# Two of four column groups of an output projection as a seven-product pair, on one Trainium2 core

## The chip, the cores and the metric

The kernel runs on one core of one Trainium2 chip. The metric is device time in microseconds (us); a median of several runs is compared. The engines are TensorE (PE in the profile), VectorE (DVE), ScalarE (ACT), GpSimd (POOL) and SyncE (SP, whose queue issues the plain loads).

## The reference

One layer of a streaming encoder on 256 tokens of width 2048 in float32: a SwiGLU block with layer norm, a mixer with two branches, a second SwiGLU block, and a gated per-layer embedding. The change lies in the last part of the mixer and touches the norm behind it:

```
merged = sigmoid(ga) * (y_m @ w_up_m) + sigmoid(gb) * (y_sb @ w_up_sb)   # (256, 2048)
mix    = merged @ w_out                                                  # w_out: 2048 x 2048
x      = layer_norm(ALPHA * x + mix)
```

## The kernel before

**Products.** Every float32 operand of a large product is cut into a high part in the fast matmul format (a cast on ScalarE, L1275) and the rest (a subtraction on VectorE, L1279); a product is then three matmuls, high by high, high by low and low by high (L1331 to L1333). A *weight* is a raw tile of 256 rows by 512 columns, loaded by SP (L1249) and split into two tiles. A *unit* is one weight against one token tile of 128 tokens, so six matmuls of 512 columns. Activations lie transposed in an `ActT`, in four chunks of 512 rows and two token tiles.

**Two ways to multiply.** `group` (L344) is the classical way: 512 output columns over all 2048 rows are eight weights, each used by two units, 16 units in all. `both7` (L420) takes two groups of 512 columns at once by `seven` (L354): in each of four quarters of the rows, a two-by-two block product (two token tiles, two column groups, two halves of rows) is made with seven products instead of eight. Each of the seven has a weight of its own with a single unit. Products 1 and 2 use the plain activations with two plain weights; products 5, 7, 6 and 3 use sums of the activations, called *forms*; 4 uses the plain ones. The weight of 5 is that of 1 plus another, made in place, that of 7 also a sum: where a quarter is in `loaded`, both are made by an accumulating load from GpSimd (L377), issued when the weight whose tile they overwrite or build on has been split. The sums for 6 and 4 are made on VectorE (L371). Results leave PSUM as sums and differences (`put`, L425, and L431).

**Forms.** An `ActT` that is built with a second one as `forms` keeps a whole copy of each transposed chunk (a second copy on ScalarE), and `form_turn` (L310) makes the sums: four half-size operations on VectorE (L315 to L319), then a cast and a subtraction for each of two tiles.

**The order.** The program is one written list of units. `Sched` holds delayed pieces of work (transposes, forms, norms) with due times in a modelled clock that advances with the units; they are put into the engines' queues between units when they come due. `weave` spreads a side list evenly by columns between the units of a main list. `skewed` puts all units of the first token tile ahead of those of the second. Splits are put out ahead of use as far as `limits` (L1231) allows: `HELD` gives for each mode how many raw tiles and how many split weights may be held. Near a boundary the limits are 4 and 11. Everything of 4 KB a partition (raw tiles, split tiles, activations, x, gates, norm weights) is a page of one pool of 51; a piece of work without a free page waits until one is given back.

**The stage.** Before the stage runs a woven part (mode "woven": 9 raw, 6 split) whose side list is of seven-product pairs, the last of them `pair(3)`, and whose main list ends with `ups(2)`. Then, in mode "mix" (6 and 6), x is brought back, the six merge turns of the first three chunks come due (`merge_turn`, L1086: transposes L298, a copy L300 and a subtraction L305), and `ups(3)`, 16 units, makes the last chunk of `merged`: `up_done` multiplies by the gate (L1079) and adds the halves (L1081). After that come four classical groups of w_out. Each result is added to ALPHA times x (L1134), with statistics for the norm (L501). The last six weights of the last group are skewed, so that the norm of the first token tile (L507 to L513, transposes L524, L292, L293) runs beside the last units of the second. Behind the boundary comes the second SwiGLU block.

Of the kernel before, what the change touches and what calls it, by code (L numbers as in the profile page):

```python
# [13 lines left out]
P = 128  # L14
S = 256
TT = S // P
D = 2048
# [6 lines left out]
COL = 512  # L24
# [2 lines left out]
TEMP_BUFS = 6  # L27


HELD = {"ffn": (11, 6), "mix": (6, 6), "woven": (9, 6), "wide": (11, 6)}  # L30
RAW_EDGE, SPLIT_EDGE = 4, 11
EDGE = 6

AHEAD = 3
PSUM_BUFS = 8
SKEW = 6

HEAD = 20

# [13 lines left out]


DELAY = {
    "alpha": 24.0, "away": 5.0, "sig": 5.0, "form": 18.0, "ln_turn": 3.6, "ln_step": 2.1, "gb": 14.0, "h": 8.0, "silu": 6.0, "late": 9.0, "last": 5.0, "rest": 1.2, "mt": 3.2,
    "sbt": 4.6, "g0": 3.0, "g1": 4.0, "g2": 12.0, "cv0": 1.0, "cv1": 5.0, "cv2": 1.3,
    "m0": 4.0, "m1": 4.0, "m2": 2.0, "m3": 4.6, "m4": 4.6, "sa": 1.4, "s0": 6.5, "s1a": 4.0, "s1": 4.5, "s2": 3.0, "s3": 5.0, "s4": 5.5,
}
# [47 lines left out]
class ActT:  # L107


    def __init__(self, alloc, forms=None, later=False):  # L110
        self.alloc, self.soon = alloc, forms is not None and not later
        self.forms, self.whole = forms, {}
        self.tiles = {}
        self.left = {}

    def get(self, c, tt):
        if (c, tt) not in self.tiles:
# [62 lines left out]
def flat(pairs):  # L180
    return [u for p in pairs for u in p]


def skewed(pairs):
    return [p[0] for p in pairs] + [p[1] for p in pairs]
# [3 lines left out]
def kernel(  # L189
# [7 lines left out]
    x, out = x[0], out[0]  # L197
# [11 lines left out]
    sched = Sched()  # L209
    temps = [0]  # L210

    def temp():
        sched.until(lambda: temps[0] < TEMP_BUFS)
        temps[0] += 1
        return temp_pool.tile([P, COL], F32, name="temp", tag="temp")

    def drop(n=1):
        temps[0] -= n
# [76 lines left out]
    def transposed(src, act, c, t):  # L295
        ps = misc([P, 4, P])
        for k in range(4):
            nc.tensor.transpose(ps[:, k], src[:, k * P:(k + 1) * P], ident[:])  # L298
        dst = act.get(c, t)
        nc.scalar.copy(dst[:, 0], ps[:])  # L300
        if act.soon:
            if c not in act.whole:
                act.whole[c] = big()
            nc.scalar.copy(act.whole[c][:, t * COL:(t + 1) * COL], ps.rearrange("q k s -> q (k s)"))  # L304
        nc.vector.tensor_tensor(out=dst[:, 1], in0=ps[:], in1=dst[:, 0], op=ALU.subtract)  # L305
        act.mark(c, t, 4)
        if act.soon and all(act.ready(c, h) for h in range(TT)):
            sched.spawn(form_turn(act, c), DELAY["form"] + 5.0 * c)

    def form_turn(act, c):  # L310

        a = [act.whole[c][:, t * COL:(t + 1) * COL] for t in range(TT)]
        s12, s34 = temp(), temp()
        l, r = slice(0, 2 * P), slice(2 * P, 4 * P)
        nc.vector.tensor_tensor(out=s12[:, l], in0=a[1][:, r], in1=a[1][:, l], op=ALU.subtract)  # L315
        nc.vector.scalar_tensor_tensor(out=s12[:, r], in0=s12[:, l], scalar=-1.0, in1=a[0][:, l],  # L316
                                       op0=ALU.mult, op1=ALU.subtract)
        nc.vector.tensor_tensor(out=s34[:, l], in0=a[0][:, l], in1=a[1][:, l], op=ALU.subtract)
        nc.vector.tensor_tensor(out=s34[:, r], in0=a[0][:, r], in1=s12[:, r], op=ALU.add)  # L319
        yield 4.0  # L320
        for h, src in enumerate((s12, s34)):
            dst = act.forms.get(c, h)
            split_psum(dst[:, 0], dst[:, 1], src.rearrange("q (k s) -> q k s", s=P))
            drop()
            act.forms.mark(c, h, 4)
# [18 lines left out]
    def group(w, rows, col0, cols, act, done):  # L344

        accs = [{} for _ in range(TT)]
        pairs = []
        for i, r in enumerate(rows):
            tile = plain(rows_of(w, r, col0, cols))
            pairs.append([Unit(tile, t, accs[t], act, r // COL, r % COL // P,  # L350
                               i == 0, i == len(rows) - 1, done) for t in range(TT)])
        return pairs
# [59 lines left out]
    def in_line(pairs):  # L412

        out = []
        for head, first, then in pairs:
            at = max(len(out) - 4, 0)
            out = out[:at] + head + out[at:] + first + then
        return out

    def both7(w, ca, cb, act, dest, ready, loaded):  # L420

        r, held = {}, {}

        def put(k, t, a, b, op):
            nc.vector.tensor_tensor(out=r[k, t], in0=a, in1=b, op=op)  # L425

        def rest():
            u = r[0, 1]
            put(0, 1, held[7], u, ALU.add)
            z = r[1, 1] = dest(1, 1)  # L430
            nc.vector.scalar_tensor_tensor(out=z, in0=u, scalar=-1.0, in1=held[5],  # L431
                                           op0=ALU.mult, op1=ALU.subtract)
            ready(1, 1)
            return
            yield

        def done(m, ps):
            held[m] = ps
            if m == 1:
                r[0, 1] = dest(0, 1)  # L440
                nc.scalar.copy(r[0, 1], ps)
            elif m == 2:
                r[0, 0] = dest(0, 0)
                nc.scalar.copy(r[0, 0], ps)
                ready(0, 0)
            elif m == 6:
                r[1, 0] = dest(1, 0)
                put(0, 1, ps, r[0, 1], ALU.add)
                put(1, 0, held[5], r[0, 1], ALU.add)
                sched.spawn(rest(), DELAY["rest"])  # L450
            elif m == 4:
                sched.until(lambda: (1, 1) in r)
                put(0, 1, ps, r[0, 1], ALU.add)
                ready(0, 1)
            elif m == 3:
                put(1, 0, ps, r[1, 0], ALU.subtract)
                ready(1, 0)

        return seven(w, ca, w, cb, D, COL, act, done, loaded)
# [3 lines left out]
    def mode(name):  # L463
        program.append(Mode(name))
# [6 lines left out]
    class Norm:  # L471
# [47 lines left out]
        def turn(self, t, c):  # L519

            xs, act = xres(t, c * COL), self.act
            ps = misc([P, 4, P])
            for k in range(4):
                nc.tensor.transpose(ps[:, k], xs[:, k * P:(k + 1) * P], ident[:])  # L524
            if act.soon:
                if c not in act.whole:
                    act.whole[c] = big()
                whole = act.whole[c][:, t * COL:(t + 1) * COL]
            else:
                whole = temp()[:]  # L530
            whole = whole.rearrange("q (k s) -> q k s", s=P)
            for k in range(4):
                i = 4 * c + k
                activate(whole[:, k], ps[:, k], ACT.Identity, scale=self.gb[:, i:i + 1], bias=self.gb[:, 16 + i:17 + i])
            dst = act.get(c, t)
            split_psum(dst[:, 0], dst[:, 1], whole)
            act.mark(c, t, 4)
            if not act.soon:
                drop()
            elif all(act.ready(c, h) for h in range(TT)):  # L540
                sched.spawn(form_turn(act, c), DELAY["form"] + 5.0 * c)
            sched.spawn(self.affine(t, c), self.wait[0] + self.wait[1] * (2 * c + t))
            return
            yield
# [512 lines left out]
            yield from stick(h)  # L1057


    mergedT = ActT(act_tile)  # L1060
    ga0 = sq0 + 3 * HS * DS
    gt = {}

# [30 lines left out]
    def ups(g, swap=False):  # L1094
        parts = [flat(group(w_up_m, range(0, HM * DM, 2 * P), g * COL, COL, ymT, up_done(g, 0, swap))),
                 flat(group(w_up_sb, range(0, HS * DS, 2 * P), g * COL, COL, ysbT, up_done(g, 1, not swap)))]
        if swap:
            parts.reverse()
        return parts[0] + parts[1]
# [12 lines left out]
    def pair(g):  # L1112
# [6 lines left out]
    mode("woven")  # L1119
    program.extend(weave(main, in_line([both7(w_in, sq0 + 2 * HS * DS, sq0 + 2 * HS * DS + COL, x1T, sv_dest, sv_ready, later),  # L1120
                                   both7(w_in, 3072, 3072 + COL, x1T, mo_dest, mo_ready, every), pair(1), pair(2), pair(3)])))
    mode("mix")
    program.append(bring_back)
    program.append(lambda: [sched.spawn(merge_turn(g, t), 1.0 + 2.0 * g + t) for g in range(3) for t in range(TT)])
    program.extend(ups(3))

    x2T = ActT(act_tile, ActT(act_tile))
    norm2 = Norm(ln2_g[0], ln2_b[0], x2T, ALPHA, (4.0, 1.0))
# [1 line left out]
    def out_done(g):  # L1130
        def done(ps, t):
            assert (t, g) in norm1.whole
            xs = xres(t, g * COL)
            nc.vector.scalar_tensor_tensor(out=xs, in0=xs, scalar=ALPHA, in1=ps, op0=ALU.mult, op1=ALU.add)  # L1134
            norm2.chunk(t, g)
        return done

    for g in range(4):
        pairs = group(w_out, range(0, D, 2 * P), g * COL, COL, mergedT, out_done(g))
        if g == 3:  # L1140
            program.extend(flat(pairs[:-SKEW]) + skewed(pairs[-SKEW:]))
        else:
            program.extend(flat(pairs))
        if g == 1:
            program.append(norm2.load)

    boundary("ffn")

# [220 lines left out]
```

## Time and profile before

| | |
|---|---|
| median of 3 runs | 2165.43 us (2164.31 to 2167.08) |
| the profiled execution | 2164.03 us |
| its span | 2162.3 us |
| instructions | 27685 |
| TensorE, VectorE, ScalarE, GpSimd busy | 2153.1, 1897.6, 1344.6, 218.2 us |

Times in the views are counted from the first instruction of the span. TensorE shows as busy nearly throughout, because its matmuls are pipelined and their ends are modelled; what it does in a stretch is read from the distance of its results. A line such as L1279 collects the splits of all stages, so stages are told apart by windows of time. In the order of time of an engine, a bracket at the end of a row tells how long the engine stood before it and what released it.

### The profile page before, as it was taken

How to read it: one execution, taken by the hardware profiler on the slowest of the kernel's cores; microseconds unless marked ns; L12 is line 12 of the kernel's file. 1: busy time of each engine (PE TensorE's matmuls, PEld its weight loads, DVE VectorE, ACT ScalarE, POOL GpSimd, SP SyncE). 2: the span in 40 equal slices, each digit the busy share in tenths (PEclk: the TensorE clock that was granted, in tenths of full speed). 3: DMA queues.
4: the chain of work that ended last, by engine and by line, in shares of the span. 5: the costliest groups of instructions: out<-in, count | busy, mean ns of one | idle time of the engine just before them, and what ended most of it. 6: DMA issues, size and time to landing. Idle time of an engine off the chain costs nothing.

```text
span 2162.3 us, 27685 instructions
## 1 busy us (share of the span) xinstructions
PE 2153.1 (100%) x9798; PEld 1782.0 (82%) x9798; DVE 1897.6 (88%) x2096; ACT 1344.6 (62%) x1663; POOL 218.2 (10%) x186
## 2 busy tenths in 40 slices
PE   9999999999999999999999999999999999999999
PEld 7888888888888888888888888888888888888887
DVE  6899999999998898887888975799999999999974
ACT  7656656666665765677866563556656656666572
POOL 0111111111000000101011000011111111110000
PEclk9999999999999999999999999999999999999999
DMA  9899899999994667978898976579989999999642
GB/s 350 220 272 271 248 269 277 273 277 269 266 316 148 211 217 217 244 212 208 263 276 264 274 259 206 200 191 277 267 245 279 277 272 270 265 273 301 233 168 86
DMA packets 283179, 535.98 MB, mean 248 GB/s; under 512 B 17144, under 2 KB 34464, under 8 KB 283040
## 3 DMA queue, kind: packets, MB, share of 16 engines
q1 hardware_dynamic: 234624, 440.87, 60.0%
q0 software_dynamic: 48416, 93.33, 24.0%
q8 instruction: 77, 1.26, 0.2%
q14 instruction: 62, 0.51, 0.1%
HBM read 527.85 MB, written 6.29 MB: 247 GB/s over the span
## 4 chain that ended last, share of the span: by engine, by line
PE 91%; DVE 4%; issue 3%; DMA 2%; ACT 0%; POOL 0%; SPq 0%; DVEq 0%; POOLq 0%; ACTq 0%
PE mm L1331 29%; PE mm L1333 29%; PE mm L1332 29%; DMA raw<-in_ffn_w_dram 2%; DVE split L1279 2%; PE ms L298 1%; PE ms L524 0%; DVE actT L293 0%; POOL raw L377 0%; DVE raw L371 0%; PE ms L911 0%; PE ms L1019 0%; PE ms L989 0%; PE ms L926 0%; ACT split L1275 0%
## 5 line engine op out<-in xcount | busy, mean ns | idle before, releaser
L1275 ACT CAST split<-raw 128x1024 fp32r<-128x1024 f32 (+1 forms) x1089 | 1089.5, 1043 | 516.9 <-DMA raw<-in_ffn_w_dram 185.8
L1279 DVE TENSOR_TENSOR split<-raw,split 128x1024 fp32r<-128x1024 f32 (+1 forms) x1089 | 1277.1, 1210 | 136.6 <-ACT split L1275 128.5
L1331 PE MATMUL mm<-split,actT 128*128 128x512 f32 x3064 | 1201.2, 392 | 0.9 <-DVE actT L1025 0.9
L1333 PE MATMUL mm<-split,actT 128*128 128x512 f32 x3064 | 1187.7, 388 | 0.6 <-DVE actT L305 0.6
L1332 PE MATMUL mm<-split,actT 128*128 128x512 f32 x3064 | 1186.1, 387 | 0.4 <-DVE split L1279 0.4
L1333 PEld LDWEIGHTS mm<-split,actT 128*128 128x128 f32 x3064 | 575.1, 188 | 121.5 <-DVE actT L305 1.8
L1331 PEld LDWEIGHTS mm<-split,actT 128*128 128x128 f32 x3064 | 575.7, 188 | 115.5 <-ACT big L243 1.1
L1332 PEld LDWEIGHTS mm<-split,actT 128*128 128x128 f32 x3064 | 575.8, 188 | 114.5 <-DVE split L1279 1.7
L377 POOL DMA_DIRECT2D raw<-in_ffn_w_dram x140 | 169.7, 1440 | 1202.8 <-DVE split L1279 780.0
L371 DVE TENSOR_TENSOR raw<-raw 128x1024 f32<-128x1024 f32 x190 | 231.4, 1219 | 1.6
L377 POOL DMA_DIRECT2D raw<-in_w_in_dram x38 | 46.0, 1428 | 502.6 <-DVE split L1279 432.8
L300 ACT CAST actT<-ms 128x512 fp32r<-128x512 f32 x60 | 35.1, 586 | 73.6 <-PE ms L298 69.2
L649 DVE SCALAR_TENSOR_TENSOR big<-mm,big 128x512 f32<-128x512 f32 x112 | 76.3, 683 | 3.3 <-PE mm L1333 3.3
L597 DVE TENSOR_TENSOR temp<-mm,temp 128x512 f32<-128x512 f32 x108 | 73.1, 686 | 1.7 <-PE mm L1333 0.3
L305 DVE TENSOR_TENSOR actT<-ms,actT 128x512 fp32r<-128x512 f32 x60 | 40.9, 685 | 14.4 <-ACT big L304 9.3
L243 ACT ACTIVATE temp<-mm 128x512 f32<-128x512 f32 (+1 forms) x36 | 20.3, 569 | 49.9 <-PE mm L1333 49.9
L293 DVE TENSOR_TENSOR actT<-temp,actT 128x512 fp32r<-128x512 f32 x40 | 26.5, 687 | 17.3 <-ACT actT L292 17.2
L239 ACT ACT_TABLE_LOAD x30 | 38.5, 1283 | 0.5
L1191 DVE TENSOR_TENSOR temp<-temp,big 128x512 f32<-128x512 f32 (+1 forms) x10 | 5.8, 582 | 26.4 <-ACT temp L243 26.4
L292 ACT CAST actT<-temp 128x512 fp32r<-128x512 f32 x40 | 23.9, 620 | 8.0 <-DVE temp L316 7.4
L243 ACT ACTIVATE rstd<-mv,eps 128x1 f32<-128x1 f32 x6 | 1.8, 294 | 41.8 <-DVE mv L507 41.8
L1134 DVE SCALAR_TENSOR_TENSOR big<-big,mm 128x512 f32<-128x512 f32 x8 | 5.5, 686 | 25.3 <-PE mm L1333 25.3
(138 smaller groups left out, 613.1 us busy)
## 6 DMA issues: line engine op xcount, KB each, us to landing
raw<-in_ffn_w_dram SPq DMA_DIRECT2D x527, 512.0 KB, 7.0
raw<-in_w_in_dram SPq DMA_DIRECT2D x144, 512.0 KB, 5.1
raw<-in_ffn_w_dram POOLq DMA_DIRECT2D x140, 512.0 KB, 9.9
raw<-in_w_in_dram POOLq DMA_DIRECT2D x38, 512.0 KB, 8.4
raw<-in_w_out_dram SPq DMA_DIRECT2D x32, 512.0 KB, 5.3
raw<-in_w_ple_gate_dram SPq DMA_DIRECT2D x32, 512.0 KB, 5.0
raw<-in_w_in_dram SPq DMA_DIRECT2D x56, 256.0 KB, 4.1
raw<-in_w_up_m_dram SPq DMA_DIRECT2D x16, 512.0 KB, 6.3
```

The costliest lines, as they stand in the source:

```text
L239: nc.scalar.preload_act_table_set(table[0])
L300: nc.scalar.copy(dst[:, 0], ps[:])
L305: nc.vector.tensor_tensor(out=dst[:, 1], in0=ps[:], in1=dst[:, 0], op=ALU.subtract)
L371: nc.vector.tensor_tensor(out=out.tile[:, :, :cols], in0=a.tile[:, :, :cols], in1=b.tile[:, :, :cols], op=ALU.add)
L377: nc.gpsimd.dma_start(out=out.tile[:, :, :cols], in_=src, accum_op=ALU.add)
L597: nc.vector.tensor_tensor(out=out, in0=a, in1=b, op=op)
L649: nc.vector.scalar_tensor_tensor(out=xs, in0=ps, scalar=0.5, in1=xs, op0=ALU.mult, op1=ALU.add)
L1275: nc.scalar.copy(hi[:, ks], r[:, ks])
L1279: nc.vector.tensor_tensor(out=lo[:, ks], in0=r[:, ks], in1=hi[:, ks], op=ALU.subtract)
L1331: nc.tensor.matmul(ps, hi, w[0][:, k, :u.cols], start=first, stop=False, skip_group_check=u.onto)
L1332: nc.tensor.matmul(ps, hi, w[1][:, k, :u.cols], start=False, stop=False, skip_group_check=u.onto)
L1333: nc.tensor.matmul(ps, lo, w[0][:, k, :u.cols], start=False, stop=last, skip_group_check=u.onto)
```

## The change

Groups 0 and 1 of w_out become one seven-product pair, all of whose quarters have their sums for products 5 and 7 made by accumulating loads (`every`). Its 28 units are woven into the main list from its thirteenth unit on, that is, after six of the eight weights of `ups(3)`; the main list is `ups(3)`, group 2, the load of the norm's weights, and the first two weights of group 3. The last six weights of group 3 stand at the end, skewed as before. `mergedT` gets forms, due 3.0 + 0.5 per chunk after a chunk's transposes instead of 18 + 5 per chunk (all others keep those). Results of the pair go to temporary tiles and from there to x. From the start of the fourth up group on, mode "out" holds up to 9 raw tiles and 11 split weights, where it was 6 and 6, and the transposes of the last chunk are due 7.0 after its sum instead of 3.2.

```diff
-HELD = {"ffn": (11, 6), "mix": (6, 6), "woven": (9, 6), "wide": (11, 6)}
+HELD = {"ffn": (11, 6), "mix": (6, 6), "woven": (9, 6), "wide": (11, 6), "out": (9, 11)}
+OUT_HEAD, OUT_FORM = 12, (3.0, 0.5)
-    "mt": 3.2,
+    "mt": 7.0,
+        self.gaps = DELAY["form"], 5.0
-            sched.spawn(form_turn(act, c), DELAY["form"] + 5.0 * c)
+            sched.spawn(form_turn(act, c), act.gaps[0] + act.gaps[1] * c)
-    mergedT = ActT(act_tile)
+    mergedT = ActT(act_tile, ActT(act_tile))
+    mergedT.gaps = OUT_FORM
-    mode("mix")
+    mode("out")
     program.append(bring_back)
     program.append(lambda: [sched.spawn(merge_turn(g, t), 1.0 + 2.0 * g + t) for g in range(3) for t in range(TT)])
-    program.extend(ups(3))
...
-    for g in range(4):
-        pairs = group(w_out, range(0, D, 2 * P), g * COL, COL, mergedT, out_done(g))
-        if g == 3:
-            program.extend(flat(pairs[:-SKEW]) + skewed(pairs[-SKEW:]))
-        else:
-            program.extend(flat(pairs))
-        if g == 1:
-            program.append(norm2.load)
+    sums = {}
+
+    def out_dest(k, t):
+        sums[k, t] = temp()
+        return sums[k, t][:]
+
+    def out_ready(k, t):
+        out_done(k)(sums[k, t][:], t)
+        drop()
+
+    last = group(w_out, range(0, D, 2 * P), 3 * COL, COL, mergedT, out_done(3))
+    main = (ups(3) + flat(group(w_out, range(0, D, 2 * P), 2 * COL, COL, mergedT, out_done(2))) + [norm2.load]
+            + flat(last[:-SKEW]))
+    side = in_line([both7(w_out, 0, COL, mergedT, out_dest, out_ready, every)])
+    program.extend(main[:OUT_HEAD] + weave(main[OUT_HEAD:], side) + skewed(last[-SKEW:]))
```

More of the change, by code (lines that the diff above doesn't have):

```diff
@@ L55 @@
 DELAY = {
-    "alpha": 24.0, "away": 5.0, "sig": 5.0, "form": 18.0, "ln_turn": 3.6, "ln_step": 2.1, "gb": 14.0, "h": 8.0, "silu": 6.0, "late": 9.0, "last": 5.0, "rest": 1.2, "mt": 3.2,
+    "alpha": 24.0, "away": 5.0, "sig": 5.0, "form": 18.0, "ln_turn": 3.6, "ln_step": 2.1, "gb": 14.0, "h": 8.0, "silu": 6.0, "late": 9.0, "last": 5.0, "rest": 1.2, "mt": 7.0,
     "sbt": 4.6, "g0": 3.0, "g1": 4.0, "g2": 12.0, "cv0": 1.0, "cv1": 5.0, "cv2": 1.3,
@@ L540, in turn @@
             elif all(act.ready(c, h) for h in range(TT)):
-                sched.spawn(form_turn(act, c), DELAY["form"] + 5.0 * c)
+                sched.spawn(form_turn(act, c), act.gaps[0] + act.gaps[1] * c)
             sched.spawn(self.affine(t, c), self.wait[0] + self.wait[1] * (2 * c + t))
```

## Prediction

> **What bounds the kernel now.** I read the page first, its busy shares and slices, then the busy time by stretches around the changed stage, and then the order of time on VectorE in that stage.
>
> ```profile
> PE 2153.1 (100%) x9798; PEld 1782.0 (82%) x9798; DVE 1897.6 (88%) x2096; ACT 1344.6 (62%) x1663; POOL 218.2 (10%) x186
> ...
> L1331 PE MATMUL mm<-split,actT 128*128 128x512 f32 x3064 | 1201.2, 392 | 0.9 <-DVE actT L1025 0.9
> ```
>
> ```profile
> 1245.00:1257.30 12.30, 12.30 (x56) 10.20 (x55) 10.01 (x11) 5.78 (x7) 0.00 (x0) 1.00 0.63 202
> 1257.30:1362.30 105.00, 105.00 (x479) 86.74 (x479) 65.61 (x70) 46.66 (x52) 0.00 (x0) 1.00 0.72 244
> 1362.30:1372.70 10.40, 10.40 (x51) 8.54 (x51) 6.00 (x11) 5.49 (x12) 0.00 (x0) 1.00 0.50 176
> 1383.00:1440.00 57.00, 57.00 (x261) 47.23 (x260) 54.73 (x73) 37.30 (x51) 4.86 (x4) 1.00 0.61 177
> ```
>
> A row of the stretches holds its bounds and length, then busy time (and count) of PE, weight loads, DVE, ACT and POOL, then the granted clock, which is 1.00, the DMA share and GB/s. TensorE is never idle, so a product that goes away is worth its whole time. The reader's second number is DVE: the changed stage (fourth up group and w_out, 1257.3 to 1362.3 up to the end of its first token tile) uses only 65.6 of 105.0 us of it, the next stage 54.7 of 57.0. So the change spends the spare time of VectorE, and what it overspends can't be paid back right behind it.
>
> ```profile
> 1258.70 0.60 PE L298 MATMUL ms<-ident,big 128*128 128x128 f32 x4
> 1303.44 0.69 DVE L1134 SCALAR_TENSOR_TENSOR big<-big,mm 128x512 f32<-128x512 f32 x1 [7.90 <-PE mm L1333]
> 1306.14 9.15 DVE L1279 TENSOR_TENSOR split<-raw,split 128x1024 fp32r<-128x1024 f32 x8
> 1325.20 0.69 DVE L1134 SCALAR_TENSOR_TENSOR big<-big,mm 128x512 f32<-128x512 f32 x1 [9.91 <-PE mm L1333]
> 1362.33 0.69 DVE L1134 SCALAR_TENSOR_TENSOR big<-big,mm 128x512 f32<-128x512 f32 x1 [6.56 <-PE mm L1333]
> ```
>
> The first results of two neighbouring groups come 1325.20 - 1303.44 = 21.76 us apart, over 16 units of six products: 1.36 us a unit, 0.2267 us a product. VectorE splits eight weights in 9.15 us (1.14 each) and then sits idle 9.91 us until TensorE finishes: TensorE sets the pace. The first transposes at 1258.70 follow the first unit, so the stage starts at about 1257.34, called T below.
>
> **What is removed.** Two classical groups are 32 units; the pair is 4 x 7 = 28. Four units of 1.36 us go: **-5.4 us**, all on the path.
>
> **What is added on VectorE.**
>
> ```profile
> 1227.54 1.22 DVE L371 TENSOR_TENSOR raw<-raw 128x1024 f32<-128x1024 f32 x1
> 1228.67 1.22 DVE L1279 TENSOR_TENSOR split<-raw,split 128x1024 fp32r<-128x1024 f32 x1
> 1235.26 0.68 DVE L425 TENSOR_TENSOR big<-mm,big 128x512 f32<-128x512 f32 x1
> 1235.86 1.22 DVE L371 TENSOR_TENSOR raw<-raw 128x1024 f32<-128x1024 f32 x1
> 1261.35 1.28 DVE L305 TENSOR_TENSOR actT<-ms,actT 128x512 fp32r<-128x512 f32 x2
> ```
>
> ```profile
> 1404.04 0.35 DVE temp L315
> 1405.51 0.81 DVE split L1279
> ```
>
> The last two rows are of the chain of waits (start, length, what): a form turn's four half-size operations take from 1404.04 to 1405.51, 1.47 us.
> - Splits: 16 weights of two units become 28 of one: 12 x 1.14 = 13.7 us.
> - Sums of weights made on VectorE (products 6 and 4; 5 and 7 come by accumulating loads): 8 x 1.13 (1227.54 to 1228.67) = 9.0 us.
> - Four form turns, 1.47 + 1.28 for two low halves: 4 x 2.75 = 11.0 us.
> - Six sums of results, taken between 0.60 (start to start at 1235.26) and 0.68: 3.9 us.
>
> Together 37.6 us. The eight updates of x and their statistics stay, from another buffer. Against it, the lead of eleven instead of six moves five splits, 5.7 us, ahead of T; there VectorE has only 12.30 - 10.01 = 2.3 us free, and the rest runs over into the stage. VectorE's work until the first token tile of w_out is done is then 65.6 + 37.6 - 2.3 = **100.9 us, in a stage that TensorE would finish in 105.0 - 5.4 = 99.6**.
>
> **The waits that are added.** All casts and splits run in program order, so one that waits for a load holds the queue.
>
> ```profile
> 1253.46 0.69 DVE L425 TENSOR_TENSOR big<-mm,big 128x512 f32<-128x512 f32 x1 [1.56 <-PE mm L1333]
> 1254.07 1.22 DVE L1279 TENSOR_TENSOR split<-raw,split 128x1024 fp32r<-128x1024 f32 x1
> 1256.66 2.00 ACT L1275 CAST split<-raw 128x1024 fp32r<-128x1024 f32 x2
> 1263.47 1.15 ACT L243 ACTIVATE big<-big 128x512 f32<-128x512 f32 x2
> 1264.82 1.07 ACT L300 CAST actT<-ms 128x512 fp32r<-128x512 f32 x2 [0.20 <-PE ms L298]
> 1188.24 2.42 POOL L377 DMA_DIRECT2D raw<-in_w_in_dram  x2 [12.55 <-DVE split L1279]
> DMA to landing us min/median/max: 7.4/9.1/10.9
> ...
> DMA to landing us min/median/max: 5.6/8.9/12.9
> ```
>
> The first landing row is that of the two accumulating loads at 1188, the second that of twenty such loads between 1000 and 1260. Product 5 of the first quarter overwrites the weight of product 1, so its load starts only when VectorE has split product 1. All quarters are loaded this way (`every`), and between the two splits VectorE has only one other split (1.14), one result (0.6) and the last up results (1.3): 3.0 us of work. With 0.2 us to issue (my allowance), landing L and a cast of 1.0 ahead of the split, VectorE stands for 0.2 + L + 1.0 - 3.0 = L - 1.8. I take 7.4, the sooner of the pair at 1188, since product 5 is issued first: 5.6 us. Behind it queue the six merge turns, the forms of the first three chunks and the splits; TensorE, eleven weights ahead, waits for them only at product 5 itself, unit 16. Likewise product 7 of the last quarter waits for its load, issued at product 6 of the third: between them lie three splits, a sum and half a form turn, 3.4 + 1.1 + 1.3 = 5.8 us, so 0.2 + L + 1.0 - 5.8 = L - 4.6, 2.8 us by the same L. Both waits are 8.4 us; at the ends, 5.6 and 12.9, they are 4.8 and 19.4. Behind the first, ScalarE has four casts, two copies for each of six merge turns and two sigmoids, 4.0 + 6 x 1.07 + 1.15 = 11.6 us, while VectorE has four splits, a sum, six low halves and the up results, 4.6 + 1.1 + 3.8 + 1.3 = 10.8: it stands another 0.8.
>
> On this the Trainium skill, "DMA: Bandwidth & Descriptors", Anatomy of one DMA, speaks the other way: a GpSimd-issued load costs about 2.0 us plus its bytes over 436 GB/s, 3.2 us for 512 KB as an estimate. This case's trace disagrees, with 5.6 as its smallest; by its figure the second wait would be gone and the first be 1.4 us.
>
> **The sum.**
>
> ```profile
> 1364.61 1.92 DVE L513 TENSOR_SCALAR big<-big,mv,rstd 128x512 f32<-128x512 f32 x4
> 1366.22 0.60 PE L524 MATMUL ms<-ident,big 128*128 128x128 f32 x4
> ```
>
> VectorE is through after 100.9 + 8.4 + 0.8 = 110.1 us instead of 99.6: 10.5 late. TensorE waits somewhere before the second norm's first transposes, in order. That norm has little slack: the first of four normalised pieces is ready about 1365.1 (1364.61 and a quarter of 1.92), its transposes start at 1366.2, so 1.1 us is forgiven. TensorE loses 10.5 - 1.1 = 9.4 and gains 5.4: **+4.0 us**. The profiled execution lasted 2164.03 us around a span of 2162.3, and the median of the runs is 2165.43, 1.4 above; 2164.0 + 4.0 is 2168.0 against that execution, and against the median it is **2169.4 us**. With L at its ends it is +0.4 and +15.0.
>
> **Edits with no cost of their own.** ScalarE gets 12 casts of 1.0, eight copies of merged tiles, eight halves of forms and two results, some 12 + 18 x 0.54 = 22 us by the rows above; with 46.7 that is 69 of 99.6 us, so it is hidden; were it not, a merge turn would add its two copies. POOL, with 0.00 busy in this stage, issues eight loads more, and the DMA share is 0.72, so the transfers fit and only their latency counts. "mt" of 7.0 moves the last chunk's transposes by some three units; product 1 of the last quarter needs them at unit 33, eight units later, 10.9 us of cover. The norm's load moves to unit 56, with 14 us of delay to its own transpose and six units to spare ahead of its first use; should its cover go, the norm starts later one for one.
>
> **The rivals.**
>
> *The lead covers it all (faster).* If the splits run far enough ahead that both waits fall into time in which VectorE has nothing to do, TensorE sees none of them: 100.9 is 1.3 late, of which 1.1 is forgiven, and some 5.4 us remain, 2160.0, or 2162.7 with half of it lost. For it: VectorE idles 39.4 us of this stage now, and the weights of the first twelve units are already split when the wait comes. Against it: forms and merge turns stand behind that wait too, and with no spare time in the stage a wait is nowhere made up. It decides if the two waits together stay under 2 us.
>
> *Short landings (near no change).*
>
> ```profile
> DMA to landing us min/median/max: 3.5/5.4/10.8
> ```
>
> This is the row of the plain raw loads from 1200 to 1400. If the accumulating loads landed like the quickest of these, 3.5 us, the first wait would be 1.7 and the second nothing: 100.9 + 1.7 + 0.8 = 103.4, 3.8 late, 3.8 - 1.1 - 5.4 = -2.7, 2162.7. With 5.6 as the shortest of twenty it gets little. The Trainium skill's rule above ("DMA: Bandwidth & Descriptors", Anatomy of one DMA) is this rival; its 3.2 us would give 2162.4.
>
> *The SBUF pages run out (slower).*
>
> ```profile
> SPq L1249 <- PE mm L1333: 120.7, 51, 9.6
> ```
>
> This row of the waits (1200 to 1400; total, times, longest) shows loads already waiting for pages that TensorE gives back. After the fourth unit the new stage wants 22 pages of split weights, 9 raw, 4 of x, 8 of the two branches, 4 of gates, 6 merged and 3 whole: 56 of 51. Five short is 2.5 weights less lead; over 52 units of 1.36 us go 40 weights, 1.77 us each, so 4.4 us more of wait, 2173.8, or 2178.2 if the late raw loads cost as much again. This is also the way in which the change does not do what it says: eleven held on paper, some eight in fact. It decides as soon as casts wait for pages while VectorE is behind.
>
> **How the numbers follow.** The forecast has 0.55, the covering lead 0.22, short landings 0.05, the lack of pages 0.18. About 0.2% (4.3 us) is what a measurement of this kernel can tell from no change. Of the forecast, +0.4 to +15.0 around +4.0, 0.25 lies within it and 0.30 above. The covering lead gives 0.20 faster and 0.02 the same, short landings 0.05 the same, the lack of pages 0.18 slower: 0.20 faster, 0.32 the same, 0.48 slower. The range reaches from the full gain, 2160.0 less 0.2 for the scatter of the runs, to 2181, just above the long latency's 2180.4; the forecast's own is 2165.8 to 2180.4.
>
> **What would show it.** Right: each of the three product lines with 3056 entries instead of 3064 (four units of six, over three lines); VectorE over 95% busy in the stage apart from one wait of 4 to 8 us near its start that ends with an accumulating load of w_out; TensorE idle or sparse in two places, near the first product 5 and ahead of the norm's transposes; the stretch from T to those transposes 4 us longer than 108.9. Wrong: TensorE without gaps and the stretch about 5 us shorter, or a stall in a place that waits for a load on SP's queue, or a gap in the next stage instead of this one.

## The result, and the profile after

| | before | after |
|---|---|---|
| median of 5 runs | 2167.03 us (2164.31 to 2168.21) | 2174.63 us (2173.27 to 2177.11) |
| ratio, 95% interval | | 1.0042 (1.003 to 1.0053) |
| the profiled execution, its span | 2164.03, 2162.3 us | 2175.94, 2174.2 us |

The change makes the kernel slower, by 7.6 us between the medians and by some 9 us by the ratio. The forecast was 2169.4 us, in a range of 2159.8 to 2181.0.

The page of the changed kernel, its first row and the first product line; then busy time by stretches, as before (bounds, length, PE, weight loads, DVE, ACT, POOL, clock, DMA share, GB/s):

```profile
PE 2152.4 (99%) x9774; PEld 1778.6 (82%) x9774; DVE 1934.1 (89%) x2146; ACT 1365.7 (63%) x1693; POOL 228.0 (10%) x194
...
L1340 PE MATMUL mm<-split,actT 128*128 128x512 f32 x3056 | 1199.0, 392 | 2.1 <-DVE big L1082 1.2
```

```profile
1269.20:1277.50 8.30, 0.04 (x2) 0.03 (x1) 2.60 (x4) 3.71 (x6) 0.00 (x0) 0.65 1.10 259
1277.50:1282.10 4.60, 4.60 (x13) 3.81 (x14) 4.60 (x6) 4.53 (x9) 0.00 (x0) 0.51 0.85 157
1260.00:1374.15 114.15, 102.61 (x455) 83.55 (x454) 99.47 (x121) 62.94 (x77) 9.73 (x8) 0.96 0.81 243
```

The products did go: 3056 instead of 3064 in each of the three product lines. But in the changed stage there is a hole: for 8.3 us TensorE does nothing (0.04 us busy), the next 4.6 us run at a granted clock of 0.51, and meanwhile VectorE and ScalarE are mostly idle too (2.60 and 3.71 of 8.30), while the DMA engines are full (1.10). Only DMA is at work, so a transfer is what everybody waits for. The third row runs from the start of the stage to the first result of the last group.

The order of time on VectorE, then ScalarE, then GpSimd, then TensorE, shows which transfer:

```profile
1245.35 14.85 DVE L1288 TENSOR_TENSOR split<-raw,split 128x1024 fp32r<-128x1024 f32 x13
1260.11 0.68 DVE L427 TENSOR_TENSOR big<-mm,big 128x512 f32<-128x512 f32 x1
1260.71 1.22 DVE L1288 TENSOR_TENSOR split<-raw,split 128x1024 fp32r<-128x1024 f32 x1
1261.84 0.68 DVE L1082 TENSOR_TENSOR big<-mm,big 128x512 f32<-128x512 f32 x1
1262.56 0.69 DVE L1084 TENSOR_TENSOR big<-big 128x512 f32<-128x512 f32 x1
1274.86 1.23 DVE L1288 TENSOR_TENSOR split<-raw,split 128x1024 fp32r<-128x1024 f32 x1 [11.61 <-ACT split L1284]
1276.01 0.68 DVE L1082 TENSOR_TENSOR big<-mm,big 128x512 f32<-128x512 f32 x1
1276.73 0.69 DVE L1084 TENSOR_TENSOR big<-big 128x512 f32<-128x512 f32 x1
...
1320.10 1.23 DVE L1288 TENSOR_TENSOR split<-raw,split 128x1024 fp32r<-128x1024 f32 x1 [0.74 <-ACT split L1284]
...
1374.15 0.69 DVE L1136 SCALAR_TENSOR_TENSOR big<-big,mm 128x512 f32<-128x512 f32 x1 [1.59 <-PE mm L1342]
```

```profile
1273.79 1.99 ACT L1284 CAST split<-raw 128x1024 fp32r<-128x1024 f32 x2 [14.41 <-DMA raw<-in_w_out_dram]
```

```profile
1260.55 4.90 POOL L379 DMA_DIRECT2D raw<-in_w_out_dram  x4 [54.78 <-DMA raw<-in_w_out_dram]
1296.17 2.42 POOL L379 DMA_DIRECT2D raw<-in_w_out_dram  x2 [30.72 <-DVE split L1288]
1310.57 2.42 POOL L379 DMA_DIRECT2D raw<-in_w_out_dram  x2 [11.98 <-DVE split L1288]
...
DMA to landing us min/median/max: 13.2/13.2/13.2
...
DMA to landing us min/median/max: 13.2/17.1/19.6
```

```profile
1261.31 0.60 PE L300 MATMUL ms<-ident,big 128*128 128x128 f32 x4
...
1268.82 0.39 PE L1342 MATMUL mm<-split,actT 128*128 128x512 f32 x1
1277.47 1.12 PE L300 MATMUL ms<-ident,big 128*128 128x128 f32 x4 [8.26 <-DVE big L1084]
1278.24 0.78 PE L1340 MATMUL mm<-split,actT 128*128 128x512 f32 x1
...
1282.12 0.40 PE L1340 MATMUL mm<-split,actT 128*128 128x512 f32 x1
```

Thirteen splits in a row, then one result, the split of the second product 1 (1260.71), the results of an up unit, and then 11.61 us of nothing. ScalarE stands 14.41 us for the load of w_out behind it. GpSimd issues four accumulating loads from 1260.55 on; the first landing row is the first of them alone, 13.2 us, the second all four, up to 19.6. So the cast of the first product 5 can start at 1273.8, and VectorE's queue moves again at 1274.9. TensorE reaches the sixth merge turn at 1269. Its transposes read the third chunk of `merged` for the second token tile, and the sum that makes this tile (L1084 at 1276.73) is queued behind the waiting split. TensorE stands 8.26 us and starts at 1277.47, just after that sum. When it goes on, a product takes (1282.12 - 1278.24) / 9 = 0.43 us instead of 0.2267.

The waits of TensorE in the stage and at the norm (1257 to 1382; total, times, longest); the kernel before has none there:

```profile
PE ms L300 <- DVE big L1084: 8.3, 1, 8.3
PE ms L300 <- DVE actT L307: 1.3, 1, 1.3
PE mm L1340 <- DVE big L1082: 1.2, 1, 1.2
PE ms L300 <- DVE big L1082: 0.8, 1, 0.8
```

From the first transposes to the first result of the last group it was 1362.33 - 1258.70 = 103.6 us; it is 1374.15 - 1261.31 = 112.8 us, 9.2 longer. (The first transposes also come 2.6 us later in the span, 1261.31 instead of 1258.70. The last pair of accumulating loads ahead of the stage is as late, 1203.35 instead of 1200.75, so that came before the changed stage.) The sum: -5.4 for the four units, +8.3 for the hole, +2.2 at the half clock (nine products by 0.2, transposes by 0.4), +3.3 for the waits of 1.2, 0.8 and 1.3 around the last chunk, where results again lie behind a row of splits: 8.4. The last 0.8 is in no wait of this list. No lateness is left at the norm, where VectorE itself now waits 1.59 us for TensorE.

### The profile page after: what moved, and what is told of

Read it like the earlier page. It is cut to its first block, busy times and chain, and to the rows that moved or that the text cites. A ratio compares the mean times of both kernels' runs of the same rounds, so it can differ in the third digit from the quotient of the medians.

```text
span 2174.2 us, 27771 instructions
## 1 busy us (share of the span) xinstructions
PE 2152.4 (99%) x9774; PEld 1778.6 (82%) x9774; DVE 1934.1 (89%) x2146; ACT 1365.7 (63%) x1693; POOL 228.0 (10%) x194
## 4 chain that ended last, share of the span: by engine, by line
PE 91%; DMA 3%; issue 3%; DVE 2%; ACT 1%; POOL 0%; SPq 0%; DVEq 0%; POOLq 0%; ACTq 0%
PE mm L1340 29%; PE mm L1342 29%; PE mm L1341 29%; DMA raw<-in_ffn_w_dram 2%; DVE split L1288 1%; PE ms L300 1%; DMA raw<-in_w_out_dram 1%; PE ms L526 0%; ACT split L1284 0%; POOL raw L379 0%; DVE raw L373 0%; PE ms L991 0%; PE ms L913 0%; PE ms L928 0%; PE ms L1021 0%
## 5 line engine op out<-in xcount | busy, mean ns | idle before, releaser
L1284 ACT CAST split<-raw 128x1024 fp32r<-128x1024 f32 (+1 forms) x1101 | 1101.6, 1043 | 533.5 <-DMA raw<-in_ffn_w_dram 185.8
L1288 DVE TENSOR_TENSOR split<-raw,split 128x1024 fp32r<-128x1024 f32 (+1 forms) x1101 | 1292.0, 1210 | 149.3 <-ACT split L1284 139.1
L373 DVE TENSOR_TENSOR raw<-raw 128x1024 f32<-128x1024 f32 x198 | 241.1, 1219 | 1.6
L307 DVE TENSOR_TENSOR actT<-ms,actT 128x512 fp32r<-128x512 f32 x60 | 40.8, 684 | 13.4 <-ACT big L306 9.5
L295 DVE TENSOR_TENSOR actT<-temp,actT 128x512 fp32r<-128x512 f32 x48 | 31.6, 687 | 17.4 <-ACT actT L294 17.3
L294 ACT CAST actT<-temp 128x512 fp32r<-128x512 f32 x48 | 28.4, 619 | 11.0 <-DVE temp L318 9.1
L245 ACT ACTIVATE temp<-ms,gbT 128x128 f32<-128x128 f32 x64 | 24.1, 460 | 5.6 <-PE ms L526 5.6
L300 PEld LDWEIGHTS ms<-ident,temp 128*128 128x128 f32 x176 | 21.4, 140 | 6.9 <-DVE actT L307 1.9
```

Source lines behind the costliest of these rows:

```text
L245: nc.scalar.activation(out, in_, func, **kw)
L373: nc.vector.tensor_tensor(out=out.tile[:, :, :cols], in0=a.tile[:, :, :cols], in1=b.tile[:, :, :cols], op=ALU.add)
L1284: nc.scalar.copy(hi[:, ks], r[:, ks])
L1288: nc.vector.tensor_tensor(out=lo[:, ks], in0=r[:, ks], in1=hi[:, ks], op=ALU.subtract)
```

## The experiments

Theory 1 was that the queues of ScalarE and VectorE stand behind the accumulating load of the first product 5; theory 2 that VectorE has too much work in the stage; theory 3 that the lead of eleven leaves too few pages. In each table row the ratio is to the kernel before, on the same chip.

| run | median, us | before beside it | ratio, 95% interval |
|---|---|---|---|
| e1 first quarter summed on VectorE | 2165.57 | 2165.14 | 1.0004 (0.9995 to 1.0012) |
| e2 lead of six | 2172.11 | 2165.14 | 1.0031 (1.002 to 1.0042) |
| e3 product 5 later | 2163.06 | 2165.14 | 0.9987 (0.9978 to 0.9996) |
| e4 lead alone, no pair | 2164.43 | 2165.14 | 0.9996 (0.9987 to 1.0004) |
| e5 e3, last transposes later | 2163.52 | 2165.19 | 0.9997 (0.9988 to 1.0006) |
| e6 e1, last transposes later | 2163.72 | 2165.19 | 0.9995 (0.9986 to 1.0004) |
| e7 x brought back later | 2168.72 | 2165.19 | 1.0019 (1.001 to 1.0028) |
| e8 third chunk's merge turns later | 2176.22 | 2165.19 | 1.0052 (1.004 to 1.0065) |
| e9 e3 with a lead of eight | 2165.51 | 2164.63 | 1.0004 (0.9995 to 1.0013) |
| e10 e3 with x later | 2161.26 | 2164.63 | 0.9981 (0.9973 to 0.999) |
| e11 e10 with a lead of eight | 2167.11 | 2164.63 | 1.0009 (1.0 to 1.0018) |

### e1: take the load away

```diff
-    side = in_line([both7(w_out, 0, COL, mergedT, out_dest, out_ready, every)])
+    side = in_line([both7(w_out, 0, COL, mergedT, out_dest, out_ready, later)])
```

> The first quarter's sums for products 5 and 7 are made on VectorE instead of by accumulating loads; the other quarters keep their loads. Theory 1 (the queues of ScalarE and VectorE stand behind the accumulating load of the first product 5, and TensorE behind them): the 11.6 us wait of VectorE, the 8.3 us stall of TensorE and the half clock behind it go, VectorE gets two sums of 1.13 more: 2161 to 2165 us, below the kernel before. Theory 2 (VectorE's total work in the stage is what is too much): 2.3 us more work, so 2175 to 2177. Theory 3 (the lead of eleven leaves too few pages, so casts and loads wait): no difference to the changed kernel, 2174 to 2175.

With 2.3 us more work for VectorE the kernel is some 8 us faster than the change (1.0004 against 1.0042). That is against theories 2 and 3 and for theory 1; but at 2165.57 it lies just above the whole range that theory 1 gave, and it is not below the kernel before. TensorE's waits in this run, 1230 to 1420:

```profile
PE mm L1340 <- DVE big L1082: 2.3, 1, 2.3
PE ms L300 <- DVE actT L307: 1.3, 1, 1.3
PE ms L300 <- DVE big L1082: 0.8, 1, 0.8
```

The hole is gone, with no half clock; 4.4 us stay around the last chunk's up results.

### e2: the lead

```diff
-"out": (9, 11)
+"out": (9, 6)
```

> The changed kernel with six held splits in the new stage instead of eleven. Theory 1: the split of the first product 5 now comes into the queue behind the merge turns and the last up results, so TensorE no longer stalls at the transposes; but the smaller lead lets later splits come just in time: 2164 to 2170 us. Theory 2: no split is made ahead, so VectorE's shortage shows more: 2175 to 2180. Theory 3: the pages suffice and the time falls to 2162 to 2165, below what the first experiment gives.

2172.11 lies in the range of none of the three theories. Its interval overlaps that of the change, so a gain over it is not shown. It speaks against theory 3, which had the time fall to 2162 to 2165. The trace is that of the slowest of seven runs (2176.90). In it the 8.3 us hole at the merge turns is gone, but TensorE stands 2.7 us at a later transpose and 3.0 us before the norm's transposes, where the prediction had expected the change itself to pay, and its clock falls in two stretches.

```profile
PE ms L526 <- DVE big L515: 3.0, 1, 3.0
PE ms L300 <- DVE actT L307: 2.7, 1, 2.7
PE mm L1341 <- DVE split L1288: 2.3, 2, 1.6
...
1300.00:1310.00 10.00, 7.29 (x27) 5.58 (x26) 9.85 (x11) 9.36 (x12) 1.67 (x2) 0.83 0.99 257
...
1370.00:1380.00 10.00, 7.01 (x23) 5.33 (x23) 6.12 (x11) 3.35 (x7) 0.00 (x0) 0.66 0.50 178
```

### e3: the same load, with work between

```diff
-    program.extend(main[:OUT_HEAD] + weave(main[OUT_HEAD:], side) + skewed(last[-SKEW:]))
+    program.extend(main[:OUT_HEAD] + side[:2] + main[OUT_HEAD:OUT_HEAD + 6]
+                   + weave(main[OUT_HEAD + 6:], side[2:]) + skewed(last[-SKEW:]))
```

> The pair's first two products 1 are put ahead of the last four up units and the first two units of group 2, and product 5 with the rest behind them: the same work and loads, but the split of the first product 5 stands six weights behind that of product 1 instead of two. Theory 1: in the queues the last up results, most merge turns and four splits fill the wait for the load: stall of TensorE below 3 us, 2163 to 2168 us. Theories 2 and 3: the same work, the same pages, 2173 to 2176.

This keeps every instruction and every load. The split of product 5 moves from two weights behind that of product 1 to six, and some other units shift by a few places with it. It turns the loss into a small gain, 0.9987. TensorE's two waits, and the landings of the accumulating loads issued from 1250 to 1264:

```profile
PE ms L300 <- DVE big L1084: 2.2, 1, 2.2
PE ms L526 <- DVE big L515: 0.3, 1, 0.3
...
DMA to landing us min/median/max: 11.1/18.4/23.4
```

The loads land nearly as late as in the change, the earliest after 11.1 us, and TensorE does not wait at the merge turns: the time is filled. So it is shown that the change was slow because product 5 stood too close behind product 1 for the load between them; the same load, limits and work in another order are not slow.

### e4: the lead alone

```diff
 (kernel before)
-    mode("mix")
+    mode("out")     # "out": (9, 11)
```

> The kernel before, with its four classical groups, and only the new limits (9 raw, 11 split) in that stage. Theories 1 and 2: no accumulating load and enough spare time on VectorE, so no difference to the kernel before, within 0.1%. Theory 3: casts or loads wait for pages, slower by 3 us or more.

No difference to the kernel before, as theories 1 and 2 had it. Holding eleven costs nothing by itself, where no forms and no pair ask for pages beside it.

### e5 and e6: the last chunk's transposes

```diff
-"mt": 7.0
+"mt": 12.0
```

> The third experiment (product 5 six weights behind product 1) with the transposes of the last merged chunk due 12.0 after its sum instead of 7.0. In that run TensorE still stood 2.2 us in front of those transposes, since the last up results lie behind a deep row of splits on VectorE. Theory 1b (what is left is this row: TensorE is asked for the transposes before the sum is through): the 2.2 us go, 2160 to 2162 us. Theory 2 (VectorE's total work): the wait only moves to a later split or to the norm, 2162.5 to 2164.

> The first experiment (first quarter summed on VectorE) with the last chunk's transposes due 12.0 after its sum. There TensorE stood 2.3 us for a bank whose up result was late, and 0.8 and 1.3 us at the transposes. Theory 1b: the last two go and the bank's wait stays, since it is not at a transpose: 2162 to 2164. Theory 2: no gain, 2165 to 2166.

In the trace of e5 the 2.2 us are gone, but 2.7 appear at a later transpose (`PE ms L300 <- DVE actT L307`), and then TensorE runs 3.4 us at the half clock. The interval, 0.9988 to 1.0006, overlaps e3's and the median lies where theory 2 put it: no gain. In e6 the two waits at transposes are gone and the bank's 2.3 us stay, as expected, but here 3.4 us of half clock follow them, which e1 does not have. Its median, 2163.72, lies in what theory 1b gave, and its interval overlaps that of e1, so no gain is shown. A due time moves such a wait; it does not shorten the row before it.

### e7: the crowd of loads

```diff
-    program.append(bring_back)
-    program.extend(main[:OUT_HEAD] + weave(main[OUT_HEAD:], side) + skewed(last[-SKEW:]))
+    program.extend(main[:OUT_HEAD] + [bring_back] + weave(main[OUT_HEAD:], side) + skewed(last[-SKEW:]))
```

> The changed kernel with x brought back from DRAM (four loads of 512 KB) behind the twelfth unit of the stage instead of at its start; all else as in the changed kernel. In the changed kernel the first accumulating load took 13.2 us while x and other loads ran. If that crowd makes the landing long: 8 to 10 us landing, TensorE's stall 3 to 5 us instead of 8.3, 2168 to 2171 us. If the four accumulating loads in a row make it long by themselves: landing above 12 us and 2173 to 2176.

```profile
1268.06 1.23 DVE L1287 TENSOR_TENSOR split<-raw,split 128x1024 fp32r<-128x1024 f32 x1 [6.42 <-ACT split L1283]
...
DMA to landing us min/median/max: 8.0/10.5/13.2
...
PE mm L1339 <- DVE big L1082: 3.2, 1, 3.2
PE ms L300 <- DVE big L1084: 3.1, 1, 3.1
```

With the same four accumulating loads in a row but without x's 2 MB beside them, the first lands after 8.0 us, VectorE waits 6.42 instead of 11.61, TensorE 3.1 instead of 8.3 at this place, and the time is 2168.72, as expected for the crowd. TensorE's other wait, at the last chunk's up results, grew from 1.2 to 3.2. The crowd, not the row of four, made 13.2 out of 8.0; e3 and e10 show it again, 11.1 with x's loads (e3) and 9.3 without (e10).

### e8: is it the bank?

```diff
-1.0 + 2.0 * g + t) for g in range(3)
+1.0 + 2.0 * g + t + (7.0 if g == 2 else 0.0)) for g in range(3)
```

> The changed kernel with the two merge turns of the third chunk due 7.0 later, so that the sixth one no longer asks for a PSUM bank that an up result behind the waiting split still holds. Theory 1 in its narrow form (the bank is the cause): TensorE's 8.3 us go and 2165 to 2168 us are left. In its wide form (the queue is the cause, the bank only where it shows first): TensorE goes on to the next thing that stands behind the waiting split, a bank for a new result or the forms for product 5, and loses nearly as much there: 2171 to 2175.

```profile
PE mm L1340 <- DVE big L1082: 7.1, 2, 3.8
...
1275.01 0.63 PE L1340 MATMUL mm<-split,actT 128*128 128x512 f32 x1 [3.31 <-DVE big L1082]
...
DVE split L1288 <- ACT split L1284: 13.7, 2, 12.4
```

2176.22, no better than the change. TensorE passes that transpose and stands 3.3 us at the next bank, whose up result is queued behind the waiting split, and then works at the half clock until 1282. The other 3.8 us come at 1302.8, at the last chunk's up results. VectorE waits 12.4 us for the load, as in the change (11.6). So the place where TensorE stops first hardly matters for the time; the standing queue is the cause. The expectation had taken the 8.3 us of the change for a wait for a bank. The trace ends them with the sum that the transposes read, so the edit moves a user of late data; whether the bank was missing too is not shown. This run came out a little above the 2175 at the top of what the wide form gave.

### e9 to e11: what is left, and a better version

```diff
 (e3)
-"out": (9, 11)
+"out": (9, 8)                                    # e9, e11
-    program.append(bring_back)
-    ... main[:OUT_HEAD] + side[:2] + main[...]
+    ... main[:OUT_HEAD] + side[:2] + [bring_back] + main[...]    # e10, e11
```

> The third experiment (product 5 six weights behind product 1) with eight held splits instead of eleven. If the 2.2 us left there come from the depth of the row of splits in front of the last up results: they shrink, 2160 to 2162 us. If VectorE's total work sets the time: the row is shorter, but splits come later to TensorE, and the time is the same or longer, 2163 to 2167.

> The third experiment with x brought back only behind the twelfth unit and the two products 1. If the crowd of loads still matters with the later product 5: landings near 8 to 10 us and 1 to 2 us less, 2160.5 to 2162 us. If the wait for the load is already filled there (VectorE stood only 2 us for casts): no difference, 2162.5 to 2164.

> Both together: the later product 5, x behind the twelfth unit, eight held splits. If neither depth nor crowd matters any more, VectorE's total work is what is left and the time is that of the third experiment or longer, 2163 to 2167; if both do, 2160 to 2161, the full gain of four units.

A smaller lead costs in both pairs, e9 against e3 (the intervals just touch) and e11 against e10 (clear of each other), and the longest wait is the norm's, 3.0 us in both: less is split ahead of the stage, and VectorE has no spare time inside it. e11 came out just above its 2163 to 2167. e10 is faster than the kernel before and the change, 0.9981, and its 2161.26 is what the crowd theory had it to be. Its TensorE never idles from T to the last group's first result, VectorE is busy 99.42 of 101.80 us, and the one wait left is the one at the norm:

```profile
1259.20:1361.00 101.80, 101.80 (x465) 84.03 (x464) 99.42 (x120) 62.80 (x77) 9.17 (x8) 1.00 0.93 282
...
PE ms L526 <- DVE big L515: 1.1, 1, 1.1
```

```profile
PE ms L526 <- DVE big L515: 3.0, 1, 3.0
```

The second row is e9's. So theory 2 has its part too, once theory 1's wait is out of the way: VectorE's work is the limit of about 1 us behind the 9 us fault.

## Why the prediction was right, and where it was not

- *Removed products, -5.4 us.* Right: 24 products fewer, and in e10, with no hole, the stretch from the first transposes to those of the norm is 1363.88 - 1260.54 = 103.3 us instead of 1366.22 - 1258.70 = 107.5. It holds the norm's wait of 1.1, so without it 5.3 went.

```profile
1260.54 0.60 PE L300 MATMUL ms<-ident,big 128*128 128x128 f32 x4
...
1363.88 0.66 PE L526 MATMUL ms<-ident,big 128*128 128x128 f32 x4 [1.07 <-DVE big L515]
```

- *VectorE's work, 100.9 us.* Right: 99.47 and 99.42 us busy in the same stretch of the change and of e10.
- *The wait at the first product 5.* Right in place and mechanism; the step that was mis-sized is L, 7.4 us taken and 13.2 measured. The prediction's own L - 1.8 gives 11.4 with it; 11.61 was measured. The landing row came from a stretch where two such loads ran, not four, and without x coming back; that x is loaded in the same microseconds stood in the program.
- *The wait at the last product 7, 2.8 us.* Wrong: VectorE waits nowhere more than 0.74 us there. The load is only placed behind the split of product 6 in the program; it reads nothing of it, so GpSimd issues it as soon as its own raw tile is there. The four loads in a row at 1260.55 show this: one of them is placed behind a split that VectorE made some 20 us later.
- *ScalarE 0.8 us behind the wait.* Not seen: VectorE runs on without idle.
- *Where TensorE stands.* Half wrong. The prediction had it at product 5 and before the norm. It stood earlier, at the sixth merge turn. The prediction put the merge turns behind the wait, but not that their transposes are TensorE's own work, come long before product 5, and read a sum from the same queue. TensorE lost so much there that VectorE was on time at the norm. In e2, e9, e10 and e11 there is a wait at the norm, as forecast.
- *"mt" at no cost.* Wrong: 0.8 and 1.3 us were lost at the last chunk's transposes. The cover of 10.9 us was counted to their user. What they wait for, an up result (L1082) and a low half (L307) behind rows of splits in VectorE's queue, was not looked at.
- *The rivals.* The pages are out for the lead alone (e4), and with the later product 5 a smaller lead is slower, not faster (e9, e11). The covering lead is what e3 and e10 make true by another order. Short landings did not come; the rule of the Trainium skill ("DMA: Bandwidth & Descriptors", Anatomy of one DMA), 3.2 us by its figures, is far from the 8.0 (e7) and 13.2 (the change) of the first load here. The same page's Issuing engines are not separate DMA queues, that loads of all engines share the same 16 DMA engines and interleave, agrees with e7: 13.2 with x's loads beside, 8.0 without.
- *The size.* +4.0 was forecast, some +9 measured, inside the range's +0.4 to +15.0 for L between 5.6 and 12.9. Here luck helped: with the measured 13.2 in both waits the prediction's own sum gives 100.9 + 11.4 + 8.6 + 0.8 - 99.6 - 1.1 - 5.4 = +15.6, above its range. The second wait, 8.6 of it, did not come; the half clock and the waits around the last chunk, 5.5 together, came without being in the sum.

## What to carry to other kernels

Before a load overwrites or adds to a tile, count the work in the in-order queue between the instruction that frees the tile and the one that needs the result; compare it with the landing time under the traffic of that very moment. In this kernel a distance of two weights did not cover 13.2 us, and with a distance of six TensorE did not wait for a load of 11.1. A lead of eleven splits did not hide the wait, because everything else stood behind the same instruction. Look for the wait's victims ahead of its reader: sums and results in the same queue that TensorE needs earlier stopped it first here. Moving two units and one group of loads, with no instruction less, turned a loss of some 9 us into a gain of 4.

## What was not expected of the hardware

In the changed kernel TensorE stopped at 1269.2 and started at 1277.5. Its granted clock fell to half 2 to 3 us after the stop, and came back only when it had worked again for some 4.5 us. Three stretches of one and two microseconds:

```profile
1270.00:1271.00 1.00, 0.00 (x0) 0.00 (x0) 0.00 (x0) 0.00 (x0) 0.00 (x0) 1.00 1.06 281
1272.00:1274.00 2.00, 0.00 (x0) 0.00 (x0) 0.00 (x0) 0.21 (x1) 0.00 (x0) 0.50 1.09 263
1282.00:1283.00 1.00, 1.00 (x6) 0.82 (x5) 1.00 (x3) 1.00 (x3) 0.00 (x0) 1.00 0.03 4
```

A hole of 8.3 us thus cost about 2 us more than itself. The length of a wait alone does not decide whether the clock falls. In e1 and in e6 TensorE stands 2.3 us at the same place, and only e6 has the half clock behind it; 0.83 over ten microseconds is 3.4 us of it. The first row is e1's, the second e6's:

```profile
1290.00:1300.00 10.00, 6.92 (x32) 5.16 (x31) 9.89 (x12) 8.01 (x10) 0.74 (x2) 1.00 0.87 253
1290.00:1300.00 10.00, 7.73 (x27) 5.86 (x27) 9.89 (x11) 7.66 (x8) 1.29 (x2) 0.83 0.96 277
```

The waits of 3.0 us at the norm in e9 and e11 left the clock at 1.00; that of 2.7 us in e5 brought 3.4 us of half clock. The Trainium skill's "TensorE: Matmul & The Clock Gate", What's actually happening, says that an idle window of about 3.4 us, which runs freely, halves the clock and a busy one restores it. The traces agree in the half, 0.50, and a window that runs freely would fit e1 beside e6. They do not agree in the 3.4 us: waits of 2.3 and 2.7 us were enough in e6 and e5.
